# A hybrid decoder layer on one core: four small moves in its order of work

## The chip, the cores and the metric

The kernel runs on one core of a Trainium2 chip. The metric is the device time of one execution in microseconds (us), given as the median of several runs. Engines are named as in the profile: PE (TensorE, matmuls), DVE (VectorE), ACT (ScalarE), POOL (GpSimd) and SP (SyncE, which here only issues DMAs).

## What is computed

One layer of a decoder trunk on 1024 positions with 1024 channels, all in float32. Cut to what matters:

```
h = rmsnorm(x);  z = h @ w_in            # columns: a value, a gate, B, C, V, merge gates A and B
a = a_val * sigmoid(a_gate)
a = silu(layernorm(causal_dwconv31(a) + bias))
y_a = a @ w_a
y_b = (B * causal_dwconv3(C * V)) @ w_b
x = x + (sigmoid(gA) * y_a + sigmoid(gB) * y_b) @ w_o
u = rmsnorm(x) @ w_up                    # gate path and value path, 2816 columns each
x = x + (gelu(causal_dwconv3(u_gate) + bias) * u_value) @ w_down
x = x + sigmoid(rmsnorm(x) @ w_pg) * (p @ w_ple)
out = rmsnorm(x)
```

## The kernel before, in words

Everything is kept transposed: channels on the 128 partitions, positions along the free dimension, in two halves H0 and H1 of 512 positions. A product of float32 is made of three matmuls: every operand is split into a high half, cast by ACT, and a low half, subtracted by DVE (`halve`, lines 128 to 131; `split`, 133), and PE sums high x high, high x low and low x high (`mm`, 144). So a weight or an operand can be used only after an instruction on ACT and one on DVE.

The projections `w_in` and `w_up` are taken in pairs of column blocks by a scheme of seven half-sized products (steps m = 1 to 7 of `Pair`, line 586) in place of eight. It needs sums of input blocks (`right_sums`, line 562, then `sum_halves`, 571) and sums of weight blocks, which are made by accumulating DMAs that POOL issues (line 226).

The order of work comes from three places. PE and SP run in the order of the program (line 342). In the first stage (line 472) and the last, ACT and DVE do too. Elsewhere the tile framework orders ACT, DVE and POOL when the kernel is compiled: it takes the instructions in the order of the program as priorities, and starts one when its inputs and its buffer are there in the framework's own estimate. Each engine then runs its list strictly in order. Nearly all buffers are slots of one pool of 54 tiles of 128 x 1024 (`slot`, line 122). The loading and splitting of weights is planned by `Loader` (line 155): `get` (261) hands out the next weight, and `advance` (272) issues those loads and those splits whose use is no more than a set number of matmul passes ahead (150 for a load of a whole weight, 100 for its split); `split_to` (256) issues splits up to a given use.

The stages that matter here, in order of time:

- The early products (lines 538 to 559). Two pairs of weights make the conformer's value and gate, first for H0, then for H1. `part(i, ks, c)` runs the operands ks of weights i and i + 1. Between the parts of H0 stands the sum over partitions `cs_mm` (line 549), from which ACT and DVE make H1's scale (551, 552) and then H1's operands (555).
- Gate products and row sums (lines 811 to 824). ACT takes the sigmoid of a gate (815), DVE multiplies (816), and for each of four rows of input blocks `right_sums` makes four sums of 512 columns on DVE: two differences into t13 (lines 565, 566) and two sums into t24 (567, 568) that start from t13. Then come the splits. The first product that needs them is the second of the first pair, with the weight w_s.
- The second convolution branch (lines 851 to 899). For jj = 0 to 3 `half_products(s_t)` makes two products of 24 matmuls. Layernorm runs beside it: after jj = 0 the mean, after jj = 1 the second sum over partitions (890 to 893) with a square root, a reciprocal and the scaled, activated and split operands `an` (894 to 899), which the loop from line 905 uses.
- The output projection and the row sums of the next norm (979 to 1022). `o_mm` makes a product, `o_add` (939) adds it to x and stores it as x1_d. In the last round (i = 3) the code after H0 allows the loads of `w_up` (1012, 1013), squares and splits the sum, and makes row 2's sums (1016); after H1 it makes row 3's (1018).
- The up projection (1054 to 1065), whose first four products use the first two weights ("r") with the plain operands (xgp); then comes the second sum over partitions (`o_rstd`, 1057) and the third product, with w_s and xgt.
- The down projection (1068 to 1101). Its inputs f and then x1 are loaded back from memory (1070, 1071), the first four weights are fetched together (1083), and their products run two operands at a time.

Of the kernel before, what the change touches and what calls it, by code (L numbers as in the profile page):

```python
# [21 lines left out]
KD = D // P  # L22
DC = 512
KC = DC // P
# [48 lines left out]
def trunk_kernel(ctx, tc, xT, pT, par, w_in, w_a, w_b, w_o, w_up, w_dn, w_ple, w_pg, outT):  # L73
# [268 lines left out]
    with tc.manual_schedule(engines={PE, SP}):  # L342
# [3 lines left out]
        def bank():  # L346
            return psp.tile([P, HB], F32, tag="ps", name="ps")
# [18 lines left out]
        def sqrt(r, ps):  # L366
            nc.scalar.activation(r, ps, AF.Sqrt, bias=eps_t[:, 0:1])
# [104 lines left out]
        with tc.manual_schedule(engines={ACT, DVE}):  # L472
            sqrt_table()
            load_p(0, H0)
            ld.fetch(1)
            load_p(1, H0)
            load_p(0, H1)
            load_p(1, H1)
            load_x(H0, range(KD))
            nc.sync.dma_start(prm, par)  # L480
            ld.fetch(4)
            load_x(H1, range(4))
            ld.fetch(6)
            load_x(H1, range(4, KD))

            split_p(0, H0)
            wple = [ld.get(False)]
            split_p(1, H0)
            split_p(0, H1)
            split_p(1, H1)  # L490
            pss = [ple(j) for j in range(3)]
            ssq = Ssq()
            for k in range(6):
                ssq.add(xr[k], H0)
            ple_out(pss[0], 0)
            for k in range(6, KD):
                ssq.add(xr[k], H0)
            cs = cs_split(ssq.acc[:, H0])
            ps = bank()
            cs_mm(ps, ones_d, cs)  # L500
            wple.append(ld.get(False))
            ple_out(pss[1], 1)
            sqrt(rstd[:, H0], ps)
            inverse(rstd[:, H0])
            ple_out(pss[2], 2)
            for j in range(3, KD):
                pss.append(ple(j))
            ld.split_to(3)
            ssq = Ssq()
            for k in range(3):  # L510
                ssq.square(xr[k], H1)
            scale_hi(H0, 0)
            scale_hi(H0, 1)
            scale_lo(H0, 0)
            ple_out(pss[3], 3)
            scale_hi(H0, 2)
            scale_lo(H0, 1)
            ssq.sum()
            ld.split_to(4)
            ple_out(pss[4], 4)  # L520
            ple_out(pss[5], 5)
            scale_hi(H0, 3)
            scale_lo(H0, 2)
            scale_lo(H0, 3)
            ld.split_to(6)
            ple_out(pss[6], 6)
            ple_out(pss[7], 7)
            for k in range(3, KD):
                ssq.square(xr[k], H1)
            ssq.sum()  # L530
            cs = cs_split(ssq.acc[:, H1])
            scale_x(H0, range(4, KD))

            nc.vector.tensor_scalar(neg_b, prm[:, _OFF["conv_b_w"] : _OFF["conv_b_w"] + KC * 3], -1.0, None, ALU.mult)
            nc.vector.tensor_scalar(neg_f, prm[:, _OFF["conv_f_w"] : _OFF["conv_f_w"] + KF * 3], -1.0, None, ALU.mult)


            ws = [ld.get() for _ in range(4)]
            pss = [[bank()] for _ in range(4)]

            def part(i, ks, c):
                for k in ks:
                    for w, ps in zip(ws[i : i + 2], pss[i : i + 2]):
                        hi, lo = hq[k, c.start]
                        mm([ps[-1]], w, k, (hi, lo), k == 0, k == KD - 1, 0, HB)

            part(0, range(4), H0)
            ps = bank()
            cs_mm(ps, ones_d, cs)
            part(2, range(4), H0)  # L550
            sqrt(rstd[:, H1], ps)
            inverse(rstd[:, H1])
            part(0, range(4, KD), H0)
            part(2, range(4, KD), H0)
            scale_x(H1, range(KD))
            for i in (0, 2):
                for ps in pss[i : i + 2]:
                    ps.append(bank())
                part(i, range(KD), H1)


        def right_sums(a0, a1, b0, b1):

            t13, t24 = slot("t13"), slot("t24")
            nc.vector.tensor_sub(t13[:, H0], a0, a1)
            nc.vector.tensor_sub(t13[:, H1], b1, a1)
            nc.vector.scalar_tensor_tensor(t24[:, H0], t13[:, H0], -1.0, b1, ALU.mult, ALU.subtract)
            nc.vector.scalar_tensor_tensor(t24[:, H1], t24[:, H0], -1.0, b0, ALU.mult, ALU.subtract)
            return t13, t24

        def sum_halves(t13, t24, name):

            out = {}
            hi, lo = split(t13, name + "s")
            out[5], out[7] = (hi[:, H0], lo[:, H0]), (hi[:, H1], lo[:, H1])
            hi, lo = split(t24, name + "t")
            out[6], out[4] = (hi[:, H0], lo[:, H0]), (hi[:, H1], lo[:, H1])
            return out
# [240 lines left out]
        rows = []  # L819
        for i in range(4):  # L820
            xa, xb = xr[i], xr[4 + i]
            r = sum_halves(*right_sums(xa[:, H0], xa[:, H1], xb[:, H0], xb[:, H1]), "hs")
            r[1], r[2], r[3] = hq[i, 0], hq[4 + i, 0], hq[4 + i, HB]
            rows.append(r)
        def load(src, name):
# [22 lines left out]
                    s_t.append(load_split(s_d[c], "s"))  # L848
        rows = live = None

        def half_products(acts):
            w = ld.get()
            out = []
            for i in range(2):
                pss = [bank(), bank()]
                for k in range(KC):
                    mm(pss, w, i * KC + k, acts[k], k == 0, k == KC - 1)
                out.append(pss)
            return out
# [10 lines left out]
        t_t = {}  # L870
        lr = slot("lrstd")
        an = []
        for jj in range(KC):
            gs.append(load_gates(KD, jj + 1) if jj < KC - 1 else load_gates(0, 0))
            for j, g, pss in zip((jj, 4 + jj), gs[jj], half_products(s_t)):
                for c, ps in zip(HALVES, pss):
                    nc.vector.tensor_mul(g[:, c], ps, g[:, c])
                t_t[j] = g
            if jj == 0:
                pm = [bank(), bank()]  # L880
                for c, ps in zip(HALVES, pm):
                    cs_mm(ps, ones_c, cs, c)
                for k in range(KC):
                    for c, ps in zip(HALVES, pm):
                        nc.vector.tensor_sub(acc[k][:, c], acc[k][:, c], ps)
                    ssq.add(acc[k])
                cs = cs_split(ssq.acc)
            if jj == 1:
                for c in HALVES:
                    ps = bank()  # L890
                    cs_mm(ps, ones_c, cs, c)
                    sqrt(lr[:, c], ps)
                    inverse(lr[:, c])
                for c in range(KC):
                    nc.vector.tensor_mul(acc[c], acc[c], lr)
                    nc.scalar.activation(
                        acc[c], acc[c], AF.Silu, scale=col("ln_g", c), bias=col("ln_b", c)
                    )
                    an.append(split(acc[c], "an"))


        m_t = {}
# [99 lines left out]
        for i in (2, 3):  # L1002
            for c in HALVES:
                for q in range(2):
                    if (i, c, q) == (3, H1, 1):
                        o_rstd(H0, cs_0)
                    o_mm(i + 4 * q, c, range(KD), True, True)
                    o_add(i, q, c)
                if c is H0:
                    o_plain(i)  # L1010
                if i == 3 and c is H0:
                    ld.held.clear()
                    ld.advance(ld.at - 1)
                    o_square(i, c)
                    cs_0 = cs_split(osum[0])
                    o_sums(2)
                elif i == 3:
                    o_sums(i)
                    o_square(i, c)
                else:  # L1020
                    o_square(i, c)
# [46 lines left out]

        while len(f_t) < DCHUNKS[0]:
            f_t.append(load_split(f_d[len(f_t)], "f"))  # L1070
        x1 = [load(x1_d[j], "x1") for j in range(KD)]
        f0 = 0
        for ci, n in enumerate(DCHUNKS):
            last = ci == len(DCHUNKS) - 1
# [5 lines left out]
            for j in range(KD):  # L1080
                if ci == 0 and j == 0:

                    ws = [ld.get() for _ in range(4)]
                    pss = [[bank(), bank()] for _ in range(4)]
                    for ks in (range(2), range(2, n)):
                        for w, ps in zip(ws, pss):
                            for k in ks:
                                mm(ps, w, k, f_t[k], k == 0, k == n - 1)
                elif j >= len(pss):
                    pss.append(product(f_t))  # L1090
# [243 lines left out]
```

## Time and profile before

| | |
|---|---|
| median of 3 runs | 1379.75 us (1375.85 to 1383.29) |
| the profiled execution | 1380.31 us |
| its span in the profile | 1378.5 us |
| PE busy | 1327.0 us, 96% |
| DVE busy | 911.2 us, 66% |
| ACT busy | 526.6 us, 38% |
| POOL busy | 181.6 us, 13% |
| DMA | 216.64 MB, mean 157 GB/s |
| chain that ended last | PE 83%, DVE 7%, issue 6% |

A row of the waits says which engine and line waited for which, how long in all, how often, and the longest. A row in order of time gives start and length in us, engine, line, operation, tiles and shape; in brackets stand the idle time before it and what ended it. The granted clock (PEclk) is given as a share of the full 2.4 GHz.

### The profile page before, as it was taken

What the parts mean: (1) busy time and instruction counts of PE and PEld (TensorE: products, weight loads), DVE (VectorE), ACT (ScalarE), POOL (GpSimd) and SP (SyncE); (2) the same over time, 40 slices, a digit from 0 to 9 for tenths busy, and PEclk for the clock granted to TensorE, in tenths of its full rate; (3) what the DMA queues carried; (4) which work ended last, traced back from release to release, by engine and by line L of the source; (5) the groups of instructions that cost most, each with busy time, mean ns of one, the idle gap of its engine ahead of it and who ended that gap; (6) DMA issues with size and microseconds to landing.
All of it is one profiled execution on the core that took longest, in us unless ns stands there. A gap on an engine that the chain in (4) does not pass through costs nothing.

```text
span 1378.5 us, 15422 instructions
## 1 busy us (share of the span) xinstructions
PE 1327.0 (96%) x5930; PEld 1102.2 (80%) x5930; DVE 911.2 (66%) x1036; ACT 526.6 (38%) x691; POOL 181.6 (13%) x247
## 2 busy tenths in 40 slices
PE   9989999999998999869999999999989999999996
PEld 7768888788887888758888888888867888887996
DVE  7869999999349755566565665656674441145777
ACT  7543333233445234334433344333444130024554
POOL 1211221122100000221222221222000000000011
PEclk9999999999999999989999999999999999999999
DMA  9645686578674413575776666776474241102222
GB/s 345 178 119 133 178 231 159 144 206 220 184 288 172 168 39 129 158 174 145 188 190 173 183 168 179 192 187 172 137 285 188 86 151 35 50 32 88 71 91 73
DMA packets 84905, 216.64 MB, mean 157 GB/s; under 512 B 9696, under 2 KB 14048, under 8 KB 84832
## 3 DMA queue, kind: packets, MB, share of 16 engines
q1 hardware_dynamic: 52992, 140.15, 30.8%
q0 software_dynamic: 31840, 75.51, 24.0%
q8 instruction: 46, 0.75, 0.2%
q14 instruction: 27, 0.22, 0.1%
HBM read 159.00 MB, written 36.70 MB: 142 GB/s over the span
## 4 chain that ended last, share of the span: by engine, by line
PE 83%; DVE 7%; issue 6%; DMA 2%; ACT 2%; POOL 1%; DVEq 0%; ACTq 0%; POOLq 0%; SPq 0%
PE ps L608 47%; PE ps L153 34%; DVE acc L683 2%; DVE w_s_lo L131 1%; DMA x<-x_d 1%; DVE sc_cv L683 1%; DMA s<-w_up 1%; PE ps L937 1%; PE ps L936 1%; PE ps L935 1%; DMA s<-w_in 0%; DVE w_r_lo L131 0%; POOL x_d L947 0%; DVE ssq L406 0%; ACT f_hi L130 0%
## 5 line engine op out<-in xcount | busy, mean ns | idle before, releaser
L683 DVE SCALAR_TENSOR_TENSOR acc<-a,prm,acc 128x1023 f32<-128x1023 f32 (+14 forms) x120 | 151.6, 1264 | 1.7
L153 PE MATMUL ps<-f_hi,whi 128*128 128x512 f32 x352 | 109.5, 392 | 5.8 <-ACT whi L130 5.8
L1094 DVE TENSOR_TENSOR x<-ps,x 128x512 f32<-128x512 f32 x46 | 29.6, 685 | 121.2 <-PE ps L153 121.2
L153 PE MATMUL ps<-f_lo,whi 128*128 128x512 f32 x352 | 109.3, 392 | 0.0
L153 PE MATMUL ps<-f_hi,wlo 128*128 128x512 f32 x352 | 108.9, 391 | 0.0
L131 DVE TENSOR_TENSOR w_s_lo<-s,w_s_hi 128x1024 fp32r<-128x1024 f32 x76 | 92.5, 1218 | 13.7 <-ACT w_s_hi L130 13.7
L630 ACT COPY u<-ps 128x512 f32<-128x512 f32 x38 | 22.4, 589 | 181.1 <-PE ps L608 181.1
L226 POOL DMA_DIRECT2D s<-s x76 | 66.1, 870 | 172.8 <-DMA s<-s 60.2
L153 PEld LDWEIGHTS ps<-f_hi,whi 128*128 128x128 f32 x352 | 66.5, 189 | 19.9 <-ACT whi L130 6.2
L608 PE MATMUL ps<-xgp_hi,w_r_hi 128*128 128x512 f32 x176 | 69.6, 395 | 11.7 <-ACT w_r_hi L130 11.7
L130 ACT CAST w_s_hi<-s 128x1024 fp32r<-128x1024 f32 x76 | 79.7, 1050 | 1.1 <-PE ps L608 0.9
L153 PEld LDWEIGHTS ps<-f_hi,wlo 128*128 128x128 f32 x352 | 66.4, 189 | 14.4 <-DVE wlo L131 0.7
L153 PEld LDWEIGHTS ps<-f_lo,whi 128*128 128x128 f32 x352 | 66.7, 189 | 14.0
L683 DVE SCALAR_TENSOR_TENSOR fg<-u_t,neg_f,fg 128x1023 f32<-128x1023 f32 (+1 forms) x44 | 56.5, 1283 | 28.4 <-ACT fg L677 27.6
L131 DVE TENSOR_TENSOR wlo<-raw,whi 128x1024 fp32r<-128x1024 f32 (+2 forms) x55 | 63.1, 1159 | 18.2 <-issue 9.4
L608 PE MATMUL ps<-xgp_hi,w_r_lo 128*128 128x512 f32 x176 | 69.4, 394 | 0.2 <-DVE w_r_lo L131 0.2
L608 PE MATMUL ps<-xgp_lo,w_r_hi 128*128 128x512 f32 x176 | 69.3, 394 | 0.0
L130 ACT CAST whi<-raw 128x1024 fp32r<-128x1024 f32 (+2 forms) x55 | 54.2, 999 | 38.4 <-PE ps L153 27.9
L608 PE MATMUL ps<-xgs_hi,w_s_hi 128*128 128x512 f32 x176 | 68.5, 389 | 0.0
L608 PE MATMUL ps<-xgs_lo,w_s_hi 128*128 128x512 f32 x176 | 68.5, 389 | 0.0
L608 PE MATMUL ps<-xgs_hi,w_s_lo 128*128 128x512 f32 x176 | 68.5, 389 | 0.0
L153 PE MATMUL ps<-xp_hi,whi 128*128 128x448 f32 (+2 forms) x192 | 61.5, 320 | 1.2 <-ACT sq L398 1.2
(263 smaller groups left out, 3322.8 us busy)
## 6 DMA issues: line engine op xcount, KB each, us to landing
s<-s POOLq DMA_DIRECT2D x76, 256.0 KB, 4.2
raw_r<-w_up SPq DMA_DIRECT2D x22, 512.0 KB, 5.2
s<-w_up SPq DMA_DIRECT2D x44, 256.0 KB, 3.0
s<-w_up SPq DMA_DIRECT2D x22, 512.0 KB, 5.7
s<-w_up POOLq DMA_DIRECT2D x44, 256.0 KB, 6.3
f_d<-v_t POOLq DMA_DIRECT2D x22, 512.0 KB, 5.9
f<-f_d SPq DMA_DIRECT2D x22, 512.0 KB, 4.6
s<-w_in SPq DMA_DIRECT2D x32, 256.0 KB, 3.3
```

The lines of the kernel that those rows point to most:

```text
L130: nc.scalar.copy(hi, src)
L131: nc.vector.tensor_sub(lo, src, f32(hi))
L153: nc.tensor.matmul(ps[:, :step], wt[:, b], xt[:, t : t + step], start=f, stop=l)
L226: nc.gpsimd.dma_start(dst, src, accum_op=ALU.add)
L608: nc.tensor.matmul(ps, wt[:, b], xt, start=f, stop=l, skip_group_check=True)
L630: nc.scalar.copy(self.e[:, H1], self.b)
L683: nc.vector.scalar_tensor_tensor(dst[:, s:], src[:, : T - s], w(k), dst[:, s:], ALU.mult, ALU.add)
L935: nc.tensor.matmul(ps, whi[:, b], hi, start=first and k == ks[0], stop=False)
L936: nc.tensor.matmul(ps, whi[:, b], lo, start=False, stop=False)
L937: nc.tensor.matmul(ps, wlo[:, b], hi, start=False, stop=last and k == ks[-1])
L1094: nc.vector.tensor_add(x1[j][:, c], ps, x1[j][:, c])
```

## The change

In the early products two operands of part 2 run before the sum over partitions instead of after it. In the row sums of the input projection the two differences (lines 565 and 566) are made by GpSimd; the row sums of the up projection stay on DVE. Layernorm's second sum, with all that follows it, moves from the end of jj = 1 to the middle of jj = 2, between the two products. In the output projection, after row 2's sums, the splits of the next two weights (the first two of the up projection) are issued. And the eight loads of x1 on SP come after the down projection's first four weight requests instead of before.

```diff
             part(0, range(4), H0)
+            part(2, range(2), H0)
             ps = bank()
             cs_mm(ps, ones_d, cs)
-            part(2, range(4), H0)
+            part(2, range(2, 4), H0)
...
-        def right_sums(a0, a1, b0, b1):
+        def right_sums(a0, a1, b0, b1, eng=nc.vector):
...
-            nc.vector.tensor_sub(t13[:, H0], a0, a1)
-            nc.vector.tensor_sub(t13[:, H1], b1, a1)
+            eng.tensor_sub(t13[:, H0], a0, a1)
+            eng.tensor_sub(t13[:, H1], b1, a1)
...
-            r = sum_halves(*right_sums(xa[:, H0], xa[:, H1], xb[:, H0], xb[:, H1]), "hs")
+            r = sum_halves(*right_sums(xa[:, H0], xa[:, H1], xb[:, H0], xb[:, H1], nc.gpsimd), "hs")
...
-        def half_products(acts):
+        def half_products(acts, between=None):
...
             for i in range(2):
+                if i and between:
+                    between()
                 pss = [bank(), bank()]
...
+        def ln_end():
+            for c in HALVES:
+                ps = bank()
+                cs_mm(ps, ones_c, cs, c)
+                sqrt(lr[:, c], ps)
+                inverse(lr[:, c])
+            for c in range(KC):
+                nc.vector.tensor_mul(acc[c], acc[c], lr)
...
+                an.append(split(acc[c], "an"))
...
-            for j, g, pss in zip((jj, 4 + jj), gs[jj], half_products(s_t)):
+            for j, g, pss in zip((jj, 4 + jj), gs[jj], half_products(s_t, ln_end if jj == 2 else None)):
...
-            if jj == 1:
...
                     o_sums(2)
+                    ld.split_to(ld.at + 2)
...
-        x1 = [load(x1_d[j], "x1") for j in range(KD)]
...
                     ws = [ld.get() for _ in range(4)]
+                    x1 = [load(x1_d[j], "x1") for j in range(KD)]
```

## Rows read from the trace of the kernel before

**Rows 1.** The page: busy time of PE, share of the span, instructions.

```profile
PE 1327.0 (96%) x5930; PEld 1102.2 (80%) x5930; DVE 911.2 (66%) x1036; ACT 526.6 (38%) x691; POOL 181.6 (13%) x247
```

**Rows 2.** Waits of PE: us in total, times, longest.

```profile
PE ps L153 <- ACT whi L130: 5.8, 1, 5.8
...
PE ps L608 <- ACT w_s_hi L130: 3.5, 1, 3.5
```

**Rows 3.** Windows: busy time of each engine, granted clock (PEclk), DMA.

```profile
core 0: us, PE busy (x) PEld busy (x) DVE busy (x) ACT busy (x) POOL busy (x), PEclk, DMA share, GB/s
40.00:44.00 4.00, 3.51 (x8) 2.42 (x9) 3.47 (x6) 1.72 (x4) 0.00 (x0) 0.57 1.04 412
89.00:95.00 6.00, 6.00 (x14) 4.74 (x15) 2.21 (x2) 0.20 (x1) 1.23 (x2) 0.50 0.57 117
426.00:430.00 4.00, 4.00 (x12) 3.10 (x11) 3.41 (x2) 2.58 (x4) 0.00 (x0) 0.57 0.73 270
...
599.00:603.00 4.00, 3.77 (x9) 2.50 (x9) 3.24 (x3) 1.42 (x2) 0.83 (x1) 0.50 1.05 224
...
622.00:1016.00 394.00, 393.73 (x1737) 326.15 (x1738) 243.59 (x272) 155.82 (x189) 75.51 (x94) 1.00 0.67 174
```

**Rows 4.** PE in order of time: around each wait, and two first uses.

```profile
40.47 0.71 PE L387 MATMUL ps<-cs,ones_d 128*128 128x512 f32 x1 [2.33 <-ACT cs L130]
...
88.99 0.79 PE L608 MATMUL ps<-hss_hi,w_s_lo 128*128 128x512 f32 x1 [0.90 <-DVE w_s_lo L131]
...
423.84 0.49 PE L387 MATMUL ps<-cs_hi,ones_c 128*128 128x512 f32 x1 [2.77 <-ACT cs_hi L130]
425.10 0.50 PE L388 MATMUL ps<-cs_lo,ones_c 128*128 128x512 f32 x1 [0.77 <-DVE cs_lo L131]
...
449.29 0.62 PE L153 MATMUL ps<-an_hi,whi 128*128 128x512 f32 x2
...
598.58 0.79 PE L608 MATMUL ps<-xgp_hi,w_r_hi 128*128 128x512 f32 x1 [11.69 <-ACT w_r_hi L130]
...
613.26 0.39 PE L608 MATMUL ps<-xgt_hi,w_s_hi 128*128 128x512 f32 x1
```

**Rows 5.** DVE in order of time, 28 to 92 us.

```profile
32.48 2.36 DVE L131 TENSOR_TENSOR wlo<-raw,whi 128x1024 fp32r<-128x1024 f32 x2 [0.26 <-ACT whi L130]
...
70.92 0.69 DVE L816 TENSOR_TENSOR a<-ps,a_sig 128x512 f32<-128x512 f32 x1 [2.36 <-ACT a_sig L815]
...
81.79 0.69 DVE L816 TENSOR_TENSOR a<-ps,a_sig 128x512 f32<-128x512 f32 x1 [0.38 <-ACT a_sig L815]
...
87.72 2.35 DVE L131 TENSOR_TENSOR w_s_lo<-s,w_s_hi 128x1024 fp32r<-128x1024 f32 x2
```

**Rows 6.** Groups of DVE, 56 to 88 us: busy us, mean ns; L566 is alike.

```profile
L565 DVE TENSOR_TENSOR t<-x_raw 128x512 f32<-128x512 f32 x4 | 2.7, 682 | 0.0
```

**Rows 7.** Waits of POOL, 56 to 88 us.

```profile
POOL s L226 <- ACT a_sig L815: 23.1, 1, 23.1
```

**Rows 8.** DVE in order of time, 385 to 480 us.

```profile
440.12 4.79 DVE L131 TENSOR_TENSOR an_lo<-acc,an_hi 128x1024 fp32r<-128x1024 f32 x4
```

**Rows 9.** DVE in order of time, 505 to 640 us.

```profile
597.61 1.23 DVE L131 TENSOR_TENSOR cs_lo<-sq,cs_hi 128x1024 fp32r<-128x1024 f32 x1 [1.17 <-ACT cs_hi L130]
598.75 2.35 DVE L131 TENSOR_TENSOR w_r_lo<-raw_r,w_r_hi 128x1024 fp32r<-128x1024 f32 x2
601.02 1.22 DVE L131 TENSOR_TENSOR w_s_lo<-s,w_s_hi 128x1024 fp32r<-128x1024 f32 x1
```

**Rows 10.** 1000 to 1060 us: ACT, SP and DVE in order of time; DMA issues.

```profile
1030.94 1.06 ACT L1046 ACTIVATE fg<-fg 128x1024 f32<-128x1024 f32 x1 [6.00 <-DVE fg L683]
1031.90 2.92 ACT L130 CAST f_hi<-f 128x1024 fp32r<-128x1024 f32 x3
...
1016.32 7.20 SPq L827 DMA_DIRECT2D x<-x_d  x8
...
1051.99 1.29 DVE L1094 TENSOR_TENSOR x<-ps,x 128x512 f32<-128x512 f32 x2 [7.29 <-PE ps L153]
...
x<-x_d SPq DMA_DIRECT2D x8, 512.0 KB, 9.6
```

More of the change, by code (lines that the diff above doesn't have):

```diff
@@ L872, in trunk_kernel @@
         an = []
+        def ln_end():
[6 more added lines that the diff above has]
+                nc.vector.tensor_mul(acc[c], acc[c], lr)
+                nc.scalar.activation(
+                    acc[c], acc[c], AF.Silu, scale=col("ln_g", c), bias=col("ln_b", c)
+                )
+                an.append(split(acc[c], "an"))
         for jj in range(KC):
             gs.append(load_gates(KD, jj + 1) if jj < KC - 1 else load_gates(0, 0))
-            for j, g, pss in zip((jj, 4 + jj), gs[jj], half_products(s_t)):
+            for j, g, pss in zip((jj, 4 + jj), gs[jj], half_products(s_t, ln_end if jj == 2 else None)):
                 for c, ps in zip(HALVES, pss):
@@ L887, in trunk_kernel @@
                 cs = cs_split(ssq.acc)
-            if jj == 1:
[L889 to L899, printed above, removed]
         m_t = {}
```

## The prediction

> **What bounds the kernel now.** I read the busy times first, then the list of who waited for whom on PE, then PE's instructions in order of time around each wait, and last the other engines in those same stretches. PE is busy for 1327.0 of 1378.5 us [rows 1], so nothing but its gaps and its slow stretches can be won. The five waits that the edits could touch are 5.8 and 3.5 us [rows 2] and 2.33, 2.77 and 11.69 us [rows 4]; two more follow at once, 0.90 us on the low half of a weight and 0.77 us on the low half of a sum [rows 4]. A wait costs more than its length: where PE runs on, a matmul of 512 columns takes 394 / 1737 = 0.227 us at granted clock 1.00, but after these waits the granted clock stands at 0.50 to 0.57 for some us (the lower of the two levels, 1.2 against 2.4 GHz), and 8, 14, 12 and 9 matmuls take 4, 6, 4 and 4 us [rows 3]. At 0.227 each they would take 1.8, 3.2, 2.7 and 2.0 us. Less the 0.5 us at 40 us that belongs to the wait itself, the clock costs 1.7, 2.8, 1.3 and 2.0 us.
>
> The sum is made against the profiled execution, 1380.3 us (span 1378.5 and 1.8 around it); it lies 0.6 above the median of 1379.75.
>
> **First stage (the early sums of H1, and two row sums by GpSimd).** Twelve matmuls of part 2 move ahead of the sum over partitions (L548 to L550). They need the first two rows and the last two weight splits, whose low halves end at 32.48 + 2.36 = 34.8 us [rows 5], before PE stops at 40.47 - 2.33 = 38.1 [rows 4]. They take 12 x 0.227 = 2.7 us, the wait was 2.3, so the sum itself starts some 0.4 us later, and the chain behind it (square root, reciprocal, scaling of H1) stays where it was within that. PE gains 2.3 and the 1.7 of clock: 4.0 us. The H1 product that follows starts 4.0 us earlier, and I cost that earlier need of H1 at nothing: DVE writes its rows ahead of PE and at about PE's pace. If that cover is gone, PE waits there for what DVE is late, at most the 4.0 us again.
>
> That gain is not kept by itself, because DVE ends last here: the first w_s split on DVE starts at 87.72 and PE goes on at 88.99 [rows 4, 5]. DVE waits 2.36 us at 70.92 and 0.38 at 81.79 for the sigmoid of a gate that PE had just finished [rows 5]. Both come 4.0 us earlier. From the last gate product to the w_s split it is 87.72 - 81.79 = 5.93 us, and this stretch holds row 3's four sums; two of them, 0.68 us each [rows 6], go to GpSimd, which leaves 4.6. Last gate product at 77.8, w_s split at 82.4: 5.3 us earlier, and PE with it. PE arrives at about 79.8 and still waits, so the slow clock behind the wait stays. **Term: 5.3.**
>
> GpSimd's price for a subtraction stands in no row. From below it is DVE's 0.68; from above, POOL stands idle for 23.1 us in this stretch [rows 7], so eight of them delay nothing queued on POOL (the accumulating loads of the next pair) up to 2.9 us each. I take about 1 us, nearer the lower row since it is the same work on the same bytes; a few tenths more are hidden, since a row's inputs are ready while DVE works on the row before. On DVE I take no loss. If DVE's order changes so that row 3 no longer stands behind the last gate product, PE wouldn't wait at all: 2.3 + 1.7 + 3.5 + 0.9 + 2.8 = 11.2. If both engines hold each other up, see the first rival. Behind the stage, DVE and PE alternate without slack till 264 us; both shift together, so I let the gain through.
>
> **Layernorm's second sum.** The four sum matmuls move behind 24 product matmuls (5.4 us at 0.227). PE stopped at 423.84 - 2.77 = 421.1 [rows 4]; at 426.5, when it now comes to the sum, both halves lie ready. Gone: 2.8 + 0.8 + 1.3 of clock = 4.9. What moves later: square root, two reciprocals, four multiplications and the splits that follow start about 1 us later; the last low half ended at 440.12 + 4.79 = 444.9 [rows 8]. PE used the first at 449.29 [rows 4], in future at about 444.4, one operand every 6 matmuls (1.4 us, so the fourth at about 448.5). The first, ready at 441.3, would be at 442.3, the fourth at 445.9: 2 us in hand. **Term: 4.9**, with 0 as the other end if the gate products slip in ahead of them on DVE.
>
> **First up weights split early.** The 11.69 us end with w_r_hi on ACT [rows 4], cast after everything of row 3 and the last sum of squares; its low half follows at 598.75 on DVE [rows 9]. The split is now asked for after row 2's sums, before the H1 products. The first four products need nothing but these two weights and the plain operands, so PE can go on at 598.58 - 11.69 = 586.9 with 48 matmuls, 10.9 us, till 597.8. Then it needs the second sum and w_s. Two splits ahead of them put DVE back by 2.35 us [rows 9]: cs_lo, which ended at 598.8, ends at 601.2; the w_s split, 602.24 before, moves little, since it lay behind the same two splits already. So w_s is there at about 602.4. The third product started at 613.26 [rows 4] and now starts at about 602.4. A wait of some 3 to 4 us stays, with 2.0 of clock: 613.3 - 602.4 - 2.0 = **8.9**. Other end above: no wait left, 11.7 + 2.0 = 13.7. Below: the four tiles of the splits must find free buffers while row sums and the SP loads of the next pairs want them too; if they find none, 0. The copies of a finished product (L617) stand in ACT's queue too, and the third product can't start without them.
>
> **x1 behind the weights.** Eight loads of SP (1016.3 to 1023.5) [rows 10] pass behind four weight loads that the same four requests issue. Their first reader is DVE at 1051.99, their landing takes 9.6 us [rows 10]; issued 4 us later they land by about 1040, so nothing is lost. But the 5.8 us wait ends with a cast of whi [rows 2] that stands on ACT behind three f_hi casts, and these behind the GELU at 1030.94, which waited 6.00 us for DVE [rows 10]. It is the third weight, and by the planner's distances its load goes out ahead of x1 already. **Term: 0**; the upper end is the wait with its clock, 5.8 + 2.0 = 7.8.
>
> **Sum**: 5.3 + 4.9 + 8.9 + 0 = 19.1; 1380.3 - 19.1 = 1361.2, or 1360.7 from the median. I say 1361.
>
> **Rivals.** First, DVE and GpSimd stop each other. No row here has GpSimd compute beside DVE. If each of the eight subtractions stands DVE still for its own length t, the stage gets only DVE's vanished idle time (2.36 + 0.38) less 8 x (t - 0.68): +2.7 at t = 0.68, -2.3 at 1.3, twice DVE's time. Midway, 0.2, is 5.1 less than my term: 1366.3. The Trainium skill says just this, in SBUF — State Buffer, section "Who interferes with whom": a DVE instruction with two SBUF inputs and a GpSimd instruction that reads SBUF take one port pair in turn, and the later one waits for the whole of the earlier. No row here shows it yet. The Trainium skill's GPSIMD Engine Reference, section "Performance versus the Vector engine", has 4497 ns for 2048 elements; a quarter of that, 1.1 us, is an estimate by that page, and would give the stage -0.6, the total 1367.1.
>
> Second, the early split doesn't happen: ACT and DVE aren't ordered by hand here, and a split without buffers stays behind row 3. Then 1361.2 + 8.9 = 1370. Against it: at that point PE has read the H0 operands for the last time, so their buffers come free just then.
>
> Third, more opens than I count: DVE's order changes in the first stage or ACT's before the down projection: 1361.2 - 5.9 = 1355, - 7.8 = 1353, both 1347.
>
> Fourth, slower: the first rival with a longer t. The stage then loses 8 x (t - 0.68) - 2.7 against 13.8 won elsewhere. It is a draw at t = 2.7 us and over 0.5% slower from 3.6; at 4 us it is 1380.3 - 13.8 + 23.9 = 1390. For it: nothing bounds t but POOL's idle time. Against: DVE's 0.68.
>
> **Chances.** My forecast 0.36, lock 0.24, no early split 0.13, more opens 0.12, lock and no early split together (1375, within 0.5%) 0.09, slower 0.06. 0.5%, 6.9 us, is about what a measurement of this kernel can tell from no change. Faster by more than that: the first four, less 0.04 for a missing split that loses a little elsewhere: 0.81. Same 0.13, slower 0.06. The range 1349 to 1372 takes in the first three with their bounds and most of the fourth; about 0.18 is left out.
>
> **What would show it.** PE without a wait at 38 us; DVE with no idle before the gate products; w_s_lo before 84 us. L565 and L566 on POOL with their length, and DVE gaps or long DVE instructions beside them if the first rival holds. No wait at L387 in layernorm, and none on an_lo. PE going on at L608 right behind L937, with a short wait at L975 in place of 11.7 us. The wait for whi before the down projection as long as before. A wait on w_r_hi that stays, POOL subtractions beyond 2 us, or a new wait in the up projection would make me wrong.

## The result and the profile after

The change brings 1373.46 us (median of 7 runs, 1369.61 to 1374.65) against 1381.90 of the kernel before in the same comparison: ratio 0.9933, 95% interval 0.9918 to 0.9948. That is 9.3 us by the ratio (7.2 to 11.3 by its interval) and 8.4 by the two medians, where I forecast 19.1; the median lies 1.5 us above the end of my range. The profiled execution took 1370.23 us, 3.2 below the median, and its span is 1368.5 against 1378.5.

The page has PE busy 3.4 us less than [rows 1]; the rest of the 10.0 us came out of waits.

```profile
PE 1323.6 (97%) x5930; PEld 1099.2 (80%) x5930; DVE 913.5 (67%) x1028; ACT 525.5 (38%) x691; POOL 192.0 (14%) x255
```

The list of PE's waits (us in total, times, longest), to be held against [rows 2]:

```profile
PE ps L153 <- ACT whi L130: 5.8, 1, 5.8
PE ps L609 <- ACT w_s_hi L130: 5.7, 1, 5.7
...
PE ps L153 <- ACT an_hi L130: 2.9, 1, 2.9
PE ps L153 <- DVE an_lo L131: 2.2, 1, 2.2
...
PE ps L153 <- DVE h_lo L462: 1.9, 1, 1.9
```

The wait for w_r_hi is gone from its top. The wait for whi before the down projection is what it was, the one for w_s_hi is longer, and three are new: h_lo, an_hi and an_lo. PE in order of time shows where they stand (compare [rows 4]):

```profile
40.98 0.50 PE L388 MATMUL ps<-cs,ones_d 128*128 128x512 f32 x1 [0.22 <-DVE cs L131]
...
65.36 0.50 PE L153 MATMUL ps<-h_lo,whi 128*128 128x512 f32 x1 [1.85 <-DVE h_lo L462]
...
87.43 0.80 PE L609 MATMUL ps<-hss_hi,w_s_hi 128*128 128x512 f32 x1 [5.68 <-ACT w_s_hi L130]
...
88.88 0.80 PE L609 MATMUL ps<-hss_hi,w_s_lo 128*128 128x512 f32 x1 [0.23 <-DVE w_s_lo L131]
...
446.81 0.79 PE L153 MATMUL ps<-an_hi,whi 128*128 128x512 f32 x2 [2.90 <-ACT an_hi L130]
449.80 1.22 PE L153 MATMUL ps<-an_lo,whi 128*128 128x512 f32 x2 [2.20 <-DVE an_lo L131]
...
601.06 0.49 PE L980 MATMUL ps<-cs_hi,ones_d 128*128 128x512 f32 x1 [1.39 <-ACT cs_hi L130]
602.32 0.50 PE L980 MATMUL ps<-cs_lo,ones_d 128*128 128x512 f32 x1 [0.77 <-DVE cs_lo L131]
...
603.12 0.40 PE L609 MATMUL ps<-xgt_hi,w_s_hi 128*128 128x512 f32 x1
```

Three of the five waits that the edits could touch are gone: at 38 us, before layernorm's second sum, and for w_r_hi. But the first two came back further on. To see what each stage kept, I cut every kernel's span at four points of PE: the start of the third matmul with w_s (88.99 before), and three moments at which PE stops, each the start of a waiting matmul less its idle time: before the last w_q product of the input projection (391.97), before the first sum over partitions of the output projection (574.57), and before the next w_q product (621.59). The lengths between them, in us:

| kernel | to w_s | to 392 | layernorm's stage, to 575 | to 622 | rest | span |
|---|---|---|---|---|---|---|
| before | 88.99 | 302.98 | 182.60 | 47.02 | 756.9 | 1378.5 |
| after | 88.88 | 303.23 | 184.67 | 34.91 | 756.8 | 1368.5 |
| differences on GpSimd alone | 89.98 | 304.44 | 182.30 | 46.31 | 755.9 | 1378.9 |
| early H1 matmuls alone | 87.95 | 303.09 | 183.26 | 46.84 | 756.8 | 1377.9 |
| layernorm's sum alone | 88.85 | 303.50 | 184.78 | 46.26 | 756.5 | 1379.9 |
| early split alone | 87.51 | 302.95 | 183.22 | 36.31 | 756.9 | 1366.9 |
| after, differences on DVE | 87.43 | 304.07 | 185.11 | 35.08 | 757.2 | 1368.9 |
| after, layernorm's order set | 90.58 | 303.11 | 178.20 | 37.55 | 757.2 | 1366.6 |
| three edits | 87.26 | 303.14 | 178.17 | 37.63 | 757.1 | 1363.3 |
| and weights asked for first | 86.97 | 303.00 | 178.16 | 37.60 | 753.7 | 1359.4 |
| and ACT's order, output sum | 87.66 | 302.81 | 178.16 | 33.22 | 754.8 | 1356.6 |
| and the fourth gate | 84.75 | 303.89 | 178.16 | 31.83 | 753.6 | 1352.2 |
| after, GpSimd writing constants | 83.04 | 301.62 | 184.81 | 34.93 | 757.1 | 1361.5 |
| after, GpSimd copying one input | 83.70 | 303.21 | 184.81 | 34.97 | 756.8 | 1363.5 |

The change got 0.1 us from the first stage (forecast 5.3), lost 2.1 in layernorm's (forecast a gain of 4.9), won 12.1 by the early split (forecast 8.9) and nothing by x1 (forecast 0). One profile's stage isn't exact: the first stage is the same code in the kernel before, with layernorm's sum alone and with the early split alone, and took 88.99, 88.85 and 87.51.

**The first stage.** DVE in order of time, 58 to 90 us:

```profile
58.98 5.72 DVE L457 SCALAR_TENSOR_TENSOR x_raw<-x_raw,prm,rstd 128x512 f32<-128x512 f32 x1
...
68.82 0.69 DVE L817 TENSOR_TENSOR a<-ps,a_sig 128x512 f32<-128x512 f32 x1 [1.19 <-ACT a_sig L816]
69.43 1.39 DVE L568 SCALAR_TENSOR_TENSOR t<-t,x_raw 128x512 f32<-128x512 f32 x1
...
72.71 2.21 DVE L131 TENSOR_TENSOR hst_lo<-t,hst_hi 128x1024 fp32r<-128x1024 f32 x1
74.84 1.77 DVE L568 SCALAR_TENSOR_TENSOR t<-t,x_raw 128x512 f32<-128x512 f32 x1
...
83.34 0.68 DVE L817 TENSOR_TENSOR a<-ps,a_sig 128x512 f32<-128x512 f32 x1
...
87.61 2.35 DVE L131 TENSOR_TENSOR w_s_lo<-s,w_s_hi 128x1024 fp32r<-128x1024 f32 x2
```

and POOL, 58 to 76 us:

```profile
58.84 1.60 POOL L566 TENSOR_TENSOR t<-x_raw 128x512 f32<-128x512 f32 x1
60.17 1.50 POOL L567 TENSOR_TENSOR t<-x_raw 128x512 f32<-128x512 f32 x1
61.42 1.49 POOL L566 TENSOR_TENSOR t<-x_raw 128x512 f32<-128x512 f32 x1
62.66 1.48 POOL L567 TENSOR_TENSOR t<-x_raw 128x512 f32<-128x512 f32 x1
...
68.97 1.30 POOL L567 TENSOR_TENSOR t<-x_raw 128x512 f32<-128x512 f32 x1
71.68 2.15 POOL L566 TENSOR_TENSOR t<-x_raw 128x512 f32<-128x512 f32 x1 [1.42 <-DVE t L569]
```

A scaling of H1's rows that takes 0.75 us elsewhere stands for 5.72, from the first of four GpSimd subtractions to 0.6 us behind the end of the fourth. PE's new wait at 65 us is for the h_lo behind it. Later instructions of DVE and of POOL are both stretched where they meet. The four long instructions of DVE take 5.72 + 1.39 + 2.21 + 1.77 = 11.1 us; elsewhere in this stretch their like take 0.75 + 0.69 + 1.23 + 0.69 = 3.4, so they cost DVE 7.7 us more. The fourth gate's product stands at 83.34 without any wait, behind this late work, and not at the forecast 77.8. What follows it, 87.61 - 83.34 = 4.3 us, is near the forecast 4.6.

**Layernorm.** In the kernel before, the square roots on ACT and the reciprocals on DVE, 420 to 446 us:

```profile
426.05 1.27 ACT L367 ACTIVATE lrstd<-ps,eps_t 128x512 f32<-128x512 f32 x2
...
426.77 6.56 DVE L370 RECIPROCAL lrstd<-lrstd 128x512 f32<-128x512 f32 x2 [0.59 <-ACT lrstd L367]
```

After the change, the square roots on ACT, then DVE in order of time, 427 to 453 us:

```profile
427.15 1.27 ACT L367 ACTIVATE lrstd<-ps,eps_t 128x512 f32<-128x512 f32 x2
...
432.84 1.29 DVE L894 TENSOR_TENSOR gate<-ps,gate 128x512 f32<-128x512 f32 x2 [3.95 <-PE ps L153]
434.05 1.22 DVE L131 TENSOR_TENSOR wlo<-raw,whi 128x1024 fp32r<-128x1024 f32 x1
435.18 6.56 DVE L370 RECIPROCAL lrstd<-lrstd 128x512 f32<-128x512 f32 x2
...
448.53 4.78 DVE L131 TENSOR_TENSOR an_lo<-acc,an_hi 128x1024 fp32r<-128x1024 f32 x4
```

The square roots start 1.1 us later than before and end at 428.4. The reciprocals need nothing else, yet start at 435.18, behind two multiplications that stand still for 3.95 us until PE has made their product. So the splits of an begin at 448.53, where [rows 8] has 440.12. The windows show what PE pays beside the two waits:

```profile
446.00:456.00 10.00, 6.99 (x20) 5.26 (x21) 7.24 (x8) 7.76 (x8) 0.00 (x0) 0.66 0.27 92
600.00:606.00 6.00, 4.18 (x17) 3.19 (x18) 4.32 (x3) 4.10 (x5) 3.13 (x5) 1.00 0.94 181
```

The granted clock (the number behind the five engines) is 0.66 from 446 to 456 us, and 1.00 from 600 to 606 us, although PE waits there too.

### The profile page after: what moved, and what is told of

It reads as the page before. It is cut to its first block, busy times and chain, and to the rows that moved or that the text cites. A ratio compares the mean times of both kernels' runs of the same rounds, so it can differ in the third digit from the quotient of the medians.

```text
span 1368.5 us, 15426 instructions
## 1 busy us (share of the span) xinstructions
PE 1323.6 (97%) x5930; PEld 1099.2 (80%) x5930; DVE 913.5 (67%) x1028; ACT 525.5 (38%) x691; POOL 192.0 (14%) x255
## 4 chain that ended last, share of the span: by engine, by line
PE 83%; DVE 10%; ACT 2%; DMA 2%; issue 2%; SPq 0%; DVEq 0%; ACTq 0%
PE ps L609 46%; PE ps L153 30%; DVE acc L684 2%; PE ps L941 2%; PE ps L940 2%; PE ps L942 2%; DVE w_s_lo L131 1%; DVE x_raw L457 1%; DMA x<-x_d 1%; DVE sc_cv L684 1%; DMA f<-f_d 1%; DVE lrstd L370 0%; DMA p_raw<-pT 0%; ACT ple_o L452 0%; DMA x_raw<-xT 0%
## 5 line engine op out<-in xcount | busy, mean ns | idle before, releaser
L131 DVE TENSOR_TENSOR w_s_lo<-s,w_s_hi 128x1024 fp32r<-128x1024 f32 x76 | 92.6, 1219 | 14.4 <-ACT w_s_hi L130 14.4
L131 DVE TENSOR_TENSOR wlo<-raw,whi 128x1024 fp32r<-128x1024 f32 (+2 forms) x55 | 62.9, 1160 | 17.4 <-issue 9.4
```

Source lines behind the costliest of these rows:

```text
L131: nc.vector.tensor_sub(lo, src, f32(hi))
```

## The experiments

**One part of the change at a time.** Four kernels are the kernel before with one part alone; each part's diff stands with the change.

*The two differences on GpSimd:*

> The kernel before with the two differences on GpSimd and nothing else. Theory (GpSimd's subtractions cost DVE at least what they save): a DVE instruction of over 3 us near 60 us, the third matmul with w_s at 88 to 91 us, against 87.5 and 89.0 in the two runs without, and the time the same as the kernel before or up to 3 us over it. Rival (my term: two instructions fewer between the last gate product and w_s): the third matmul near 86.5 us, the time 1 to 3 us below the kernel before.

1382.83 us against 1381.44, ratio 1.0008 (1.0000 to 1.0017); third matmul at 89.98. DVE, 59 to 69 us:

```profile
59.67 8.57 DVE L457 SCALAR_TENSOR_TENSOR x_raw<-x_raw,prm,rstd 128x512 f32<-128x512 f32 x1
```

The same scaling stands for 8.57 us, this time across six subtractions. The theory holds: GpSimd's subtractions cost DVE at least what they save it.

*The twelve early matmuls of H1:*

> The kernel before with the twelve early matmuls of H1 and nothing else. Theory (the wait at 38 us goes, but the framework now puts the third gate's sigmoid and multiplication ahead of row 0's splits, where ACT and DVE wait for PE): the w_s split starts at about 86.2 us, against 86.2 to 87.7 in the runs without; the time is 0 to 2 us below the kernel before. Rival (my step for this part, 4.0 us): the split starts near 83.7 us, the time is 4 us below.

1379.74 us against 1381.57, ratio 0.9987 (0.9978 to 0.9996), so 1.8 us of my 4.0. DVE, 62 to 90 us:

```profile
67.13 0.69 DVE L817 TENSOR_TENSOR a<-ps,a_sig 128x512 f32<-128x512 f32 x1 [2.77 <-ACT a_sig L816]
...
78.15 0.69 DVE L817 TENSOR_TENSOR a<-ps,a_sig 128x512 f32<-128x512 f32 x1
...
86.67 2.35 DVE L131 TENSOR_TENSOR w_s_lo<-s,w_s_hi 128x1024 fp32r<-128x1024 f32 x2
```

The third gate's product comes 70.92 - 67.13 = 3.8 us earlier than in [rows 5], near the forecast 4.0. But it now stands after two of row 0's six instructions instead of after all of them, in an order that the framework made anew, and DVE waits 2.77 us there. The fourth likewise: 86.67 - 78.15 = 8.52 us of DVE's work lie behind it, where I had 5.93. The theory holds.

*Layernorm's second sum half a product later:*

> The kernel before with layernorm's second sum half a product later and nothing else. Theory (with DVE's order as the framework makes it the move costs more than it saves): the stage from 392 to 577 us, 182.6 us long before, takes 184 to 185.5, with waits of 2.9 and 2.2 us on an; the time is 1 to 3 us over the kernel before. Rival (my term): the stage takes about 178, the time is 4 to 5 us below.

1381.83 us against 1381.57, ratio 1.0004 (0.9995 to 1.0013). The stage takes 184.78 us, with waits of 2.9 and 2.3 on an: the theory's stage. The time it gave, 1 to 3 us over, isn't shown: the interval reaches from 0.7 below to 1.8 above. The rival's 4 to 5 us below are excluded.

*The early split:*

> The kernel before with one line added, the early split of the next two weights after row 2's sums. Theory (this split alone brought what the trace shows behind 577 us): the wait of 11.69 us for w_r_hi goes, waits of 1 to 2.5 us in all stay before the third product, which starts at about 610 instead of 622.3 us by the point where the 100th matmul after it is done; 12 us won, span about 1366.5. Rival (the gain came partly from the 2.2 us by which PE arrived later at this point): about 9 to 10 us won, span 1368.5 to 1369.5.

1369.11 us against 1380.65, ratio 0.9917 (0.9904 to 0.9931): 11.5 us (9.5 to 13.3 by the interval), at least about as much as the whole change. The stage to 622 takes 36.31 us instead of 47.02, 10.7 less, between the theory's 12 and the rival's 9 to 10. PE's wait that is left:

```profile
598.24 0.49 PE L975 MATMUL ps<-cs_hi,ones_d 128*128 128x512 f32 x1 [1.39 <-ACT cs_hi L130]
```

It is 1.39 us and another 0.77 for cs_lo, the same as after the change, although PE gets to this stage at 573.68 instead of 576.78. So the late arrival did not shorten the waits. The 1.4 us between 36.31 and 34.91 is mostly the clock behind them: from 600 to 604 us it stands at 0.70 here and at 1.00 after the change, and from the end of the first of these waits to 622 it takes 11.75 us here (609.99 - 598.24) and 10.63 there. This kernel still loads x1 first, and its wait for whi is 5.78 us, as it is after the change: x1's place is worth 0.

**What of GpSimd's work stops DVE.** In the changed kernel, the differences back on DVE:

```diff
-            r = sum_halves(*right_sums(xa[:, H0], xa[:, H1], xb[:, H0], xb[:, H1], nc.gpsimd), "hs")
+            r = sum_halves(*right_sums(xa[:, H0], xa[:, H1], xb[:, H0], xb[:, H1]), "hs")
```

> The changed kernel with the two differences of the row sums back on DVE; the other edits stay. Theory (GpSimd's subtractions hold DVE up): DVE has no instruction of over 2 us on 512 columns around 59 us, the wait of 1.85 us at 65 us on h_lo is gone, and the third matmul of the product with w_s starts at about 86.3 us instead of 88.9, since the 2.7 us that the first wait's end gave are kept; the span ends about 2.5 us earlier, near 1366, with the clock as it falls adding or taking 1.5. Rival (the long instruction and the late w_s come from the earlier H1 product, not from GpSimd): the third matmul stays at 88.9 us or later, a DVE instruction of some 5 us is still there, the span is 1368 or more.

1371.28 us against 1380.65, ratio 0.9929 (0.9915 to 0.9942), no different from the change. The long instruction and the wait at 65 us are gone, so GpSimd was their cause. But the third matmul starts at 87.43, between theory and rival: DVE idles 2.82 us before the third gate, and 86.16 - 77.64 = 8.5 us of its work stand behind the fourth, as with the early matmuls alone. So taking GpSimd away gave back little here, because DVE's order is another one too. Then GpSimd writes a constant and reads nothing:

```diff
+                eng.memset(t13[:, H0], 0.5)
+                eng.memset(t13[:, H1], 0.5)
```

> The changed kernel in which GpSimd only writes a constant into the tiles of the differences and reads nothing; it leaves out the two differences of every row sum of the input projection. Theory (DVE and GpSimd hold each other up by what GpSimd reads): no DVE instruction on 512 columns from 56 to 88 us takes over 0.9 us, and the third matmul with w_s starts near 83.6 us, 5.3 before that of the kernel before, as my first term had it. Rival (any GpSimd instruction beside DVE costs DVE its time): DVE still has instructions of 1.4 us and more beside GpSimd's, and the third matmul starts after 86 us.

No DVE instruction of this size takes over 0.75 us from 56 to 88 us, and the third matmul starts at 83.04. Time 1363.19 us against 1380.65, ratio 0.9871 (0.9857 to 0.9884). DVE, 56 to 88 us:

```profile
77.84 0.69 DVE L821 TENSOR_TENSOR a<-ps,a_sig 128x512 f32<-128x512 f32 x1 [0.66 <-ACT a_sig L820]
...
81.76 2.36 DVE L131 TENSOR_TENSOR w_s_lo<-s,w_s_hi 128x1024 fp32r<-128x1024 f32 x2 [0.23 <-ACT w_s_hi L130]
```

The theory holds, and it is the key to this stage. Without GpSimd's reads, and with every other edit in place, the third matmul starts 88.99 - 83.04 = 5.9 us earlier than in the kernel before, where my term was 5.3; the fourth gate's product stands at 77.84 (forecast 77.8) with 81.76 - 77.84 = 3.9 us behind it. It is a best case, since the constants wait for no row. And with one input read:

```diff
+                eng.tensor_copy(t13[:, H0], a0)
+                eng.tensor_copy(t13[:, H1], b1)
```

> The changed kernel in which GpSimd copies one input into the tile of each difference, so that it reads one tile instead of two; it leaves out the differences of the row sums of the input projection. Theory (any read by GpSimd holds DVE up): a DVE instruction near 59 us stands for 3 us or more across GpSimd's first copies, and the third matmul with w_s starts after 86 us. Rival (only two inputs read at once hold it up): every DVE instruction on 512 columns from 56 to 88 us stays under 0.9 us, and the third matmul starts near 83.5 us as with the constant.

A single run took 1365.3 us. DVE, 58 to 63 us:

```profile
58.91 3.37 DVE L457 SCALAR_TENSOR_TENSOR x_raw<-x_raw,prm,rstd 128x512 f32<-128x512 f32 x1
```

Reading one tile stops DVE too, across four copies of 0.92 us. The second half of that expectation failed: the third matmul starts at 83.70. A copy is short, so the burst is. DVE's four long instructions here lose some 3.7 us, and most of that falls into time in which DVE stood idle with the constants (1.53 + 0.24 + 0.66 us). So a hold costs the stage only what goes beyond DVE's waits.

**Layernorm with DVE's order set by hand.** In the changed kernel (`issue_after` puts what its block issues behind the named instruction on that engine):

```diff
-                    nc.vector.tensor_mul(g[:, c], ps, g[:, c])
+                    if j == 6:
+                        with tc.issue_after(recs[-1].ins):
+                            nc.vector.tensor_mul(g[:, c], ps, g[:, c])
```

> The changed kernel with the two gate multiplications of the product after layernorm's second sum put behind the second reciprocal on DVE by hand. Theory (the move is good, but those two multiplications, which wait for PE, stood ahead of the reciprocals on DVE): the waits of 2.90 and 2.20 us on an_hi and an_lo go, or leave under 1 us together, the last low half of an ends before 446 us instead of 453, the stage wins 5 to 7 us, span 1361 to 1363. Rival (half a product later is too late for PE whatever DVE's order): a wait of 2 us or more on an stays, the span is 1367 or more.

1367.35 us against 1380.65, ratio 0.9896 (0.9880 to 0.9911). DVE, 427 to 451 us:

```profile
431.51 6.56 DVE L884 RECIPROCAL lrstd<-lrstd 128x512 f32<-128x512 f32 x2
437.98 0.63 DVE L898 TENSOR_TENSOR gate<-ps,gate 128x512 f32<-128x512 f32 x1
...
444.86 1.22 DVE L131 TENSOR_TENSOR an_lo<-acc,an_hi 128x1024 fp32r<-128x1024 f32 x1
```

The multiplication stands behind the reciprocals, and PE's wait on an is 0.20 us. The stage takes 178.20 us, 6.5 under the change and 4.4 under the kernel before: the theory holds there, and this is close to my term of 4.9. The rival, that half a product later is too late in any order, falls. The span misses its 1361 to 1363: this profile's first stage is 1.7 us longer, with a wait of 1.65 at 8 us that the other lacks, and the stage to 622 is 2.6 longer, with the clock at 0.52 from 577 to 582 us.

**The first stage with its order set by hand.** The differences back on DVE, layernorm as above, and the third gate behind row 0 on DVE. `gate(c, i)` issues a gate's sigmoid and multiplication; in the program both gates of H1 now stand behind row 0's sums:

```diff
+            if i == 1:
+                with tc.issue_after(low[-1].ins):
+                    gate(0, 1)
```

> The changed kernel with three edits: the differences back on DVE, layernorm's two gate multiplications behind the second reciprocal, and the third gate multiplication of the first stage (the one before which DVE stood still for 2.82 us while four instructions of row 0 could have run) behind row 0's last split. Theory (what is left of the early operands of H1 was lost to the order on DVE): no idle time over 0.5 us on DVE from 62 us to the w_s split, which starts near 83.4 us instead of 86.2, third matmul with w_s near 84.7; no wait for an; span 1368.5 - 1.4 - 2.8 - 6.5 = 1357.8, give or take 2. Rival (the w_s split hangs on PE or on ACT there): it still starts after 85.5 us, span 1361 or more.

1364.29 us against 1381.44, ratio 0.9872 (0.9858 to 0.9886), but the w_s split starts at 85.98: the rival. ACT, 65 to 68 us (two lines added ahead moved L131 to L133):

```profile
65.95 0.60 ACT L818 ACTIVATE a_sig<-ps 128x512 f32<-128x512 f32 x1 [4.68 <-PE ps L155]
66.44 1.04 ACT L132 CAST hss_hi<-t 128x1024 fp32r<-128x1024 f32 x1
```

The sigmoid still stood ahead of row 0's casts, and DVE waits 2.38 us for them instead. The next kernel adds, for the wait before the down projection, an earlier request for its weights:

```diff
+        ws = [ld.get() for _ in range(4)]
         while len(f_t) < DCHUNKS[0]:
             f_t.append(load_split(f_d[len(f_t)], "f"))
...
-                    ws = [ld.get() for _ in range(4)]
```

> The kernel with the three edits, and in the down projection the four weights are asked for before the last two loads of f, so that ACT casts the third weight behind one cast of f instead of three. Theory (the wait for the third weight hangs on ACT's order, not on when x1 is loaded): the wait falls from 5.78 us by two casts, 1.9 us, to 3.9, span about 2 us below that of the three edits. Rival (the f operands or the weight's landing are as late): the wait moves to f_hi or f_lo and the span stays within 0.7 us.

1361.94 us against 1381.44, ratio 0.9861 (0.9846 to 0.9876). The wait is 3.89 us as expected, so it hangs on ACT's order. The span fell by 3.9: the rest of the kernel behind 622 takes 753.7 us instead of 757.1. Of these 3.4 us, 1.9 are the wait; where the others come from I did not trace. Then the sigmoid too, and the sum of squares:

```diff
-                with tc.issue_after(low[-1].ins):
+                with tc.issue_after(low[-1].ins), tc.issue_after(high[-1].ins):
                     gate(0, 1)
...
+            with tc.issue_after(sqs[-1].ins) if (i, q, c) == (3, 0, H1) else nullcontext():
                 nc.vector.tensor_add(r[:, h], obank[j, c.start], r[:, h])
```

> The kernel with the three edits and the earlier weights of the down projection, with two orders more set by hand: the sigmoid of the third gate behind row 0's last cast on ACT (before, only DVE was told to wait with its multiplication, and ACT's sigmoid, which waits for PE, still stood ahead of row 0's casts), and in the output projection the last sum of squares of H0 ahead of the addition that waits for PE. Theory (the first stage hangs on that sigmoid; the 2.99 us wait at 571 us on that addition): DVE has no idle time over 0.5 us from 62 us to the w_s split, which starts near 83.5 us instead of 86.0, the third matmul with w_s near 84.8; the wait for cs_hi falls to under 1 us; span 1359.4 - 2.4 - 2.3 = 1354.7, give or take 2. Rival (PE or the weights hold it): w_s after 85.5, or the wait of 2.99 stays, span 1358 or more.

1357.70 us against 1381.57, ratio 0.9823 (0.9810 to 0.9837). The wait for cs_hi falls from 2.99 to 0.66 us, but the w_s split starts at 86.38. DVE, 60 to 90 us:

```profile
77.85 0.69 DVE L819 TENSOR_TENSOR a<-ps,a_sig 128x512 f32<-128x512 f32 x1 [2.69 <-ACT a_sig L818]
```

Row 0 no longer waits; the fourth gate does, ahead of row 2's last three instructions. In this kernel and the others with the differences on DVE it was the fourth gate that counted, since the end is its time plus what lies behind it. The last kernel puts it behind row 2:

```diff
-                gate(1, 1)
+            if i == 3:
+                with tc.issue_after(low[-1].ins), tc.issue_after(high[-1].ins):
+                    gate(1, 1)
```

> The kernel of the run before with one order more: the sigmoid and the multiplication of the fourth gate behind row 2's last splits on ACT and DVE. In the run before they stood ahead of row 2's last three instructions and waited there 2.69 us for PE, so that 8.53 us of DVE's work lay behind them, against 5.93 in the kernel before. Theory (the early operands of H1 are worth what I forecast once both gates stand where they stood before the change): no idle time over 0.5 us on DVE from 62 us to the w_s split, which starts near 83.8 us, third matmul near 85; span 1356.6 - 2.6 = 1354.0. Rival (PE's products hold it, whatever the order): the split starts after 85.5 us and the span stays at 1356 or more.

1354.62 us against 1381.17, ratio 0.9811 (0.9797 to 0.9825). DVE, 60 to 90 us:

```profile
77.95 0.68 DVE L819 TENSOR_TENSOR a<-ps,a_sig 128x512 f32<-128x512 f32 x1
...
83.48 2.35 DVE L133 TENSOR_TENSOR w_s_lo<-s,w_s_hi 128x1024 fp32r<-128x1024 f32 x2
```

No idle time before the gate, and 83.48 - 77.95 = 5.53 us of work behind it. The third matmul starts at 84.75: the theory holds, and this is the fastest kernel here, ahead of the kernel before and the changed one.

## Why the prediction was wrong

- **First stage, 5.3 forecast, 0.1 measured.** The step "On DVE I take no loss" failed: GpSimd held DVE up, my first rival, and DVE lost 7.7 us. That used up the eight subtractions that DVE no longer makes (8 x 0.60 us from start to start, 4.8) and the idle time that it no longer has (1.2 us from 58 us on, against 3.8 before). The rest of the step was sound: behind the last gate product were 4.3 us (forecast 4.6), and without GpSimd's reads the stage gives 5.9.
- **The rival's 0.2 came out partly by luck.** It lets DVE stand still for a subtraction's whole length. In a burst they start 1.25 us apart, by which its sum would be 2.74 - 8 x (1.25 - 0.68) = -1.8; but DVE lost only 7.7 / 8 = 0.97 us for each.
- **GpSimd's price.** I took 1 us for a subtraction. It took 1.29 to 1.30 where DVE gave way, 1.48 to 1.60 in a burst and 2.15 and 2.27 in turns, beyond the 2 us that I had named as a sign of being wrong. For the DVE instruction caught first the price is not one subtraction but the burst.
- **DVE's order in that stage.** With the differences on DVE another step of mine would have failed, that "87.72 - 81.79 = 5.93 us" stay behind the last gate product: they became 8.5. In the changed kernel this was not the loss. The early matmuls are worth about what I said where both gates are set behind ready work: 84.75 against 87.5 to 89.0, so 2.8 to 4.2 us of my 4.0.
- **Layernorm, 4.9 forecast, -2.1 measured.** The step "square root, two reciprocals, four multiplications and the splits that follow start about 1 us later" failed. It held for the square roots (1.1 us), but the reciprocals came 435.18 - 426.77 = 8.4 us later: DVE's order again. I had named this ("if the gate products slip in ahead of them on DVE") and put its other end at 0. That end was too kind: with PE's work moved ahead, the operands themselves became the next wait, 5.1 us and its slow clock. With the order set, the stage gave 4.4.
- **Early split, 8.9 forecast, 12.1 measured (10.7 alone; 11.5 by the ratio).** The mechanism was right, and the second rival, that it would not happen, fell. I left "a wait of some 3 to 4 us" and 2.0 us of clock; the waits were 1.39 + 0.77 = 2.2, and the clock took from nothing to about 1.4. So the term was too small by 3.2 in the changed kernel.
- **x1, 0 forecast, 0 measured**, and the reason given, ACT's order, was the right one: a change of that order alone took 1.9 us from the wait.
- **The sum.** The first stage lost 5.2 of its term and layernorm 7.0, and the split's 3.2 more hid a part of that: 1361.2 + 5.2 + 7.0 - 3.2 = 1370.2, the profiled execution. That the total is not further off is luck. A lost layernorm gain had no chance of its own in my list, so I had no place for it together with the lock. Why the median lies 3.2 us above the profiled execution, I did not find.

## What to carry to other kernels

Where a scheduler orders an engine from its own estimate, a move on another engine can change that order, and the cost of the move is read from the new order, not from the old one: look which instruction that waits for the moved work stands ahead of work that is ready. If the gain does not show, pin the waiting instruction, on every engine of its chain (here ACT's sigmoid as well as DVE's multiplication). An engine is not free help because it is idle: before work goes from DVE to GpSimd, measure what DVE's instructions beside it take, and set that against DVE's idle time.

## What the runs showed of the hardware

Where GpSimd instructions that read SBUF followed each other without a gap, a DVE instruction with two inputs in SBUF stood not for one of them but for all: 5.72 us across four subtractions, 8.57 across six, 3.37 across four copies. Where they came one by one (from 71 us on in the changed kernel), the two engines took turns. With GpSimd writing only, no DVE instruction was stretched. The third gate's product (one input in PSUM) at 68.82 took its usual 0.69 us beside a subtraction. The Trainium skill, SBUF — State Buffer, section "Who interferes with whom", has GpSimd's reads as what a DVE instruction with two SBUF inputs contends with, writes alone as harmless, and a DVE instruction with one SBUF input as untouched. The runs agree with all three. That page of the Trainium skill lets the later instruction wait for the whole of the earlier. The turns fit this; in the bursts DVE waited for all that was queued, so the measurement goes further. In two of these three bursts the profile even has DVE's instruction start first, by 0.20 us (six subtractions) and 0.24 us (copies), though starts on POOL are rough.

The granted clock fell behind some waits and not behind others of the same length: behind 1.39 and 0.77 us before the third up product it was 1.00 after the change, the higher of its two levels, and 0.70 on average from 600 to 604 us with the split alone, with a part at the lower one. I did not find which of the two to expect. The last of these stages differs by 1.4 us between the two kernels, mostly for this, which is why the stages above were read from several kernels.
